# Gamma in four pieces on four partitions, issued beside ScalarE's table load, in an RMSNorm and SiLU kernel

## Chip, cores and metric

The kernel runs on one core of a Trainium2 chip. The metric is the device time of one execution in microseconds (us). Runs of one kernel mostly agree within half a per cent, so each kernel is run several times, in rounds with the kernel before on the same chip. A ratio below compares the fast runs of one kernel with the fast runs of the kernel before in the same rounds, so it is not quite the ratio of the medians quoted; the interval behind it is 95%. With one core a run counts as slow when it is over 1.5% above the fastest of the same kernel. A profiled span is about 1.8 us shorter than the time that the same execution is given.

## The reference

```python
# x: 8 x 1024 x 2048 float32, gamma: 2048 float32
rms = np.sqrt(np.mean(x ** 2, axis=-1, keepdims=True) + eps)
out = gamma * x / rms
return out * (1 / (1 + np.exp(-out)))
```

67.1 MB come in and 67.1 MB go out. Gamma is 8 KB, and every one of the 128 partitions needs a copy of it.

## The kernel before

x is cut into 16 blocks of 128 partitions x 4 rows of 2048 (4.19 MB, 32 KB a partition). Six buffers turn: a block is loaded, scaled in place and stored from the same buffer. Loads are issued by SyncE (SP), stores by ScalarE (ACT). For each block VectorE sums the squares of one row and ScalarE those of three, VectorE makes the inverse root and multiplies by gamma, ScalarE applies SiLU. Gamma arrives as one row on partition 0, in a buffer that the sixth load reuses; TensorE multiplies a column of ones by it, and VectorE copies the result from PSUM, where the matmuls leave it, to a buffer g that every later multiplication reads.

```python
def store(b):
    nc.scalar.dma_start(out=ob[b], in_=blocks[b])
    if b + LEAD < nblk:
        load(b + LEAD)            # LEAD = BUFS = 6: load b+6 waits for store b
...
with tc.manual_schedule():
    grow = pool.tile([P, J * d], f32, name="xt")
    nc.scalar.dma_start(out=grow[0:1, 0:d], in_=...gamma as one row...)
    for b in range(min(LEAD, BUFS - 1)):
        load(b)
    nc.vector.memset(ones, 1.0)                       # ones is 1 x 128
    for c in range(0, d, 512):
        nc.tensor.matmul(junk_v[:, c:c + 512], ones, grow[0:1, c:c + 512], start=True, stop=True)
    nc.vector.tensor_copy(out=g, in_=junk_v)
    load(BUFS - 1)
    ...
    sums(0); rstds[0] = rsqrt(sss[0]); finish(0)
    sums(1); rstds[1] = rsqrt(sss[1])
    for b in range(1, last - 1):
        sums(b + 1, after_first=[b - 1])              # store b-1 goes out after the first sum of block b+1
        finish(b)
        rstds[b + 1] = rsqrt(sss[b + 1])
```

Of the kernel before, what the change touches and what calls it, by code (L numbers as in the profile page):

```python
# [1 line left out]

# [4 lines left out]

ACT = mybir.ActivationFunctionType
ALU = mybir.AluOpType


@with_exitstack
def kernel(
    ctx: ExitStack,
    tc: tile.TileContext,
    x: bass.AP,
    gamma: bass.AP,
    eps: bass.AP,
    out: bass.AP,
):  # L20





    nc = tc.nc
    P = nc.NUM_PARTITIONS
    f32, i32 = mybir.dt.float32, mybir.dt.int32
    x2 = x.flatten_outer_dims()
    o2 = out.flatten_outer_dims()  # L30
    n, d = x2.shape
    J = 4
    BUFS, LEAD = 6, 6
    nblk = n // (P * J)
    xb = x2.rearrange("(b p j) d -> b p (j d)", p=P, j=J)
    ob = o2.rearrange("(b p j) d -> b p (j d)", p=P, j=J)

    singles = ctx.enter_context(tc.tile_pool(name="singles", bufs=1))
    pool = ctx.enter_context(tc.tile_pool(name="pool", bufs=BUFS))
    small = ctx.enter_context(tc.tile_pool(name="small", bufs=2))  # L40
    psum = ctx.enter_context(tc.tile_pool(name="psum", bufs=1, space=bass.MemoryType.PSUM))

    g = singles.tile([P, d], f32)
    ones = singles.tile([1, P], f32)
    junk_a = psum.tile([P, d], f32, name="junk_a")
    junk_v = psum.tile([P, d], f32, name="junk_v")
    blocks, sss, rstds = {}, {}, {}

    def load(b):
        xt = pool.tile([P, J * d], f32, name="xt")  # L50
        nc.sync.dma_start(out=xt, in_=xb[b])
        blocks[b] = xt

    def row(b, j):
        return blocks[b][:, j * d:(j + 1) * d]

    def rsqrt(ss):


        var = small.tile([P, J], f32, name="var")  # L60
        nc.vector.tensor_scalar(out=var, in0=ss, scalar1=1.0 / d, scalar2=float(eps),  # L61
                                op0=ALU.mult, op1=ALU.add)
        y = small.tile([P, J], f32, name="y")
        t = small.tile([P, J], f32, name="t")
        nc.vector.tensor_single_scalar(out=t.bitcast(i32), in_=var.bitcast(i32), scalar=1,  # L65
                                       op=ALU.logical_shift_right)
        nc.vector.tensor_scalar(out=y.bitcast(i32), in0=t.bitcast(i32), scalar1=-1, scalar2=0x5F375A00,  # L67
                                op0=ALU.mult, op1=ALU.add)
        for _ in range(3):
            nc.vector.scalar_tensor_tensor(out=t, in0=y, scalar=-0.5, in1=y, op0=ALU.mult, op1=ALU.mult)  # L70
            nc.vector.tensor_mul(out=t, in0=t, in1=var)  # L71
            nc.vector.scalar_tensor_tensor(out=y, in0=t, scalar=1.5, in1=y, op0=ALU.add, op1=ALU.mult)  # L72
        return y

    def sums(b, after_first=()):


        ss = small.tile([P, J], f32, name="ss")
        nc.vector.tensor_tensor_reduce(  # L79
            out=junk_v, in0=row(b, J - 1), in1=row(b, J - 1), scale=1.0, scalar=0.0,  # L80
            op0=ALU.mult, op1=ALU.add, accum_out=ss[:, J - 1:J])
        for j in range(J - 1):
            nc.scalar.activation(out=junk_a, in_=row(b, j), func=ACT.Square,  # L83
                                 accum_out=ss[:, j:j + 1])
            if j == 0:
                for s in after_first:
                    store(s)
        sss[b] = ss

    def finish(b, pieces=1):  # L90
        for j in range(J):
            nc.vector.tensor_mul(out=row(b, j), in0=row(b, j), in1=g)  # L92
            nc.scalar.activation(out=row(b, j), in_=row(b, j), func=ACT.Silu,  # L93
                                 scale=rstds[b][:, j:j + 1])
            if pieces > 1 and (j + 1) % (J // pieces) == 0:
                w = J // pieces * d
                i = (j + 1) // (J // pieces) - 1
                nc.scalar.dma_start(out=ob[b][:, i * w:(i + 1) * w], in_=blocks[b][:, i * w:(i + 1) * w])  # L98
# [4 lines that stand above are left out]
            load(b + LEAD)  # L103

    with tc.manual_schedule():
        grow = pool.tile([P, J * d], f32, name="xt")
        nc.scalar.dma_start(out=grow[0:1, 0:d],
                            in_=bass.AP(tensor=gamma.tensor, offset=gamma.offset, ap=[[d, 1], gamma.ap[0]]))
        for b in range(min(LEAD, BUFS - 1)):
            load(b)  # L110
        nc.vector.memset(ones, 1.0)  # L111
        for c in range(0, d, 512):
            nc.tensor.matmul(junk_v[:, c:c + 512], ones, grow[0:1, c:c + 512], start=True, stop=True)  # L113
        nc.vector.tensor_copy(out=g, in_=junk_v)  # L114
        load(BUFS - 1)


        last = nblk - 1
        sums(0)
        rstds[0] = rsqrt(sss[0])  # L120
        finish(0)
        sums(1)
        rstds[1] = rsqrt(sss[1])
        for b in range(1, last - 1):
            sums(b + 1, after_first=[b - 1])
            finish(b)
            rstds[b + 1] = rsqrt(sss[b + 1])
        store(last - 2)
        finish(last - 1)
        store(last - 1)  # L130
        sums(last)
        rstds[last] = rsqrt(sss[last])
        finish(last, pieces=2)


# [1 line left out]
_INS = ['x', 'gamma', 'eps']  # L137
_OUTS = [((8, 1024, 2048), 'float32')]

_NUMBERS = {'eps': 9.999999747378752e-06}  # L140


# [26 lines left out]
```

## Time and profile before

| | before |
|---|---|
| time, median of the first 3 runs | 317.92 us (317.8 to 318.91) |
| DMA share between 80 and 240 us | 1.00, at 432 to 433 GB/s |
| busy: VectorE, ScalarE, TensorE | 66%, 70%, 2% |
| gamma in PSUM / in g / first used | 9.7 / 12.0 / 21.6 us |
| first load landed / first store issued | 13.2 / 38.48 us |

The table is read from top to bottom as "what is full, what is early": the transfers are full, and gamma is ready 9.5 us ahead of its first use. The lines themselves stand in the prediction.

### The profile page before, as it was taken

The page shows a single profiled execution, that of the slowest core. Times are in us where ns is not written, and L with a number is a line of the kernel's source. Part 1 is how long each engine was busy: PE and PEld are TensorE (multiplying, and loading weights), DVE is VectorE, ACT ScalarE, POOL GpSimd, SP SyncE. Part 2 cuts the span into 40 slices and gives each one's busy share as a digit, 9 for nine tenths or more (in the row PEclk, how much of TensorE's full clock was granted, in tenths as well). Part 3 has the DMA queues.
Part 4 walks back from the last instruction along what each step waited for, and adds up shares of the span by engine and source line. Part 5 has one row for each costly group of instructions (what it writes and reads, how often), then busy time and mean ns, then how long its engine had stood idle before and what let it go on. Part 6 is the DMA issues. An engine that isn't in the chain of part 4 may idle for free.

```text
span 317.5 us, 603 instructions
## 1 busy us (share of the span) xinstructions
PE 7.2 (2%) x8; PEld 2.5 (1%) x8; DVE 210.3 (66%) x290; ACT 221.3 (70%) x162; POOL 0.2 (0%) x4
## 2 busy tenths in 40 slices
PE   6200000000000000000000000000000000000000
PEld 2000000000000000000000000000000000000000
DVE  0559299999892947839287392974929559946600
ACT  1359989999892947939388393984929659794800
POOL 0000000000000000000000000000000000000000
DMA  8999999999999999999999999999999999999994
GB/s 327 429 433 433 425 392 455 405 454 417 442 430 433 425 438 425 433 446 425 438 425 439 417 442 433 425 458 417 442 417 446 413 446 433 430 446 425 438 411 204
DMA packets 4758, 134.26 MB, mean 423 GB/s; under 512 B 529, under 2 KB 529, under 8 KB 529
## 3 DMA queue, kind: packets, MB, share of 16 engines
q1 hardware_dynamic: 2304, 67.11, 49.4%
q10 hardware_dynamic: 2450, 67.12, 49.0%
q14 instruction: 4, 0.03, 0.0%
HBM read 67.12 MB, written 67.11 MB: 423 GB/s over the span
## 4 chain that ended last, share of the span: by engine, by line
DMA 73%; DVE 11%; ACT 7%; issue 3%; DVEq 1%; ACTq 0%; SPq 0%
DMA xt<-in_x_dram 39%; DMA out_dram<-xt 34%; DVE xt L92 8%; ACT junk_a L83 5%; ACT xt L93 3%; DVE junk_v L79 1%; DVEq L164 1%; DVE t L70 0%; DVE t L71 0%; DVE y L72 0%; DVE t L65 0%; DVE y L67 0%; DVE var L61 0%; ACTq L98 0%; ACTq L101 0%
## 5 line engine op out<-in xcount | busy, mean ns | idle before, releaser
L92 DVE TENSOR_TENSOR xt<-xt,g 128x2048 f32<-128x2048 f32 x64 | 142.3, 2285 | 0.0
L83 ACT ACTIVATE junk_a<-xt 128x2048 f32<-128x2048 f32 x48 | 90.3, 1881 | 65.5 <-DMA xt<-in_x_dram 64.0
L93 ACT ACTIVATE xt<-xt,y 128x2048 f32<-128x2048 f32 x64 | 124.0, 1992 | 13.0 <-DVE xt L92 13.0
L79 DVE CUSTOM_DVE_ANT_0 junk_v<-xt 128x2048 f32<-128x2048 f32 x16 | 36.8, 2299 | 57.5 <-DMA xt<-in_x_dram 57.5
L61 DVE TENSOR_SCALAR var<-ss 128x4 f32<-128x4 f32 x16 | 2.6, 166 | 15.7 <-ACT junk_a L83 15.7
L83 ACT ACTIVATION_READ_ACCUMULATOR junk_a<-xt 128x1 f32 x48 | 9.0, 187 | 0.0
L72 DVE SCALAR_TENSOR_TENSOR y<-t,y 128x4 f32<-128x4 f32 x48 | 7.8, 162 | 1.7
L70 DVE SCALAR_TENSOR_TENSOR t<-y 128x4 f32<-128x4 f32 x48 | 7.8, 162 | 1.7
L71 DVE TENSOR_TENSOR t<-t,var 128x4 f32<-128x4 f32 x48 | 7.8, 162 | 1.6
L114 DVE COPY g<-junk_v 128x2048 f32<-128x2048 f32 x1 | 2.3, 2292 | 8.7 <-PE junk_v L113 8.7
L113 PE MATMUL junk_v<-xt,ones 1*128 1x512 f32 x8 | 7.2, 1072 | 2.5 <-DMA xt<-in_gamma_dram 2.5
L67 DVE TENSOR_SCALAR y<-t 128x4 int32<-128x4 int32 x16 | 2.7, 170 | 0.5
L65 DVE TENSOR_SCALAR t<-var 128x4 int32<-128x4 int32 x16 | 2.7, 170 | 0.5
L113 PEld LDWEIGHTS junk_v<-xt,ones 1*128 1x128 f32 x8 | 2.5, 325 | 5.6 <-issue 5.6
L79 DVE DVE_READ_ACCUMULATOR2_ANT ss<- 128x1 f32 x16 | 2.3, 142 | 0.0
L83 ACT ACT_TABLE_LOAD x1 | 1.3, 1283 | 1.3 <-PEq L150 1.3
L93 ACT ACT_TABLE_LOAD x1 | 1.3, 1283 | 0.0
L111 DVE MEMSET ones<- 1x128 f32 x1 | 0.2, 165 | 0.8 <-PEq L150 0.8
L150 POOL MEMSET const-bfloat16-1.0<- 128x1 bf16 x1 | 0.1, 102 | 0.0
L150 POOL MEMSET const-uint8-127<- 128x1 uint8 x1 | 0.1, 102 | 0.0
L150 POOL MEMSET const-float32-0.0<- 128x1 f32 x1 | 0.1, 100 | 0.2 <-issue 0.2
L150 POOL MEMSET const-float32-1.0<- 128x1 f32 x1 | 0.1, 99 | 0.0
## 6 DMA issues: line engine op xcount, KB each, us to landing
xt<-in_x_dram SPq DMA_DIRECT2D x16, 4096.0 KB, 36.8
out_dram<-xt ACTq DMA_DIRECT2D x15, 4096.0 KB, 40.6
out_dram<-xt ACTq DMA_DIRECT2D x2, 2048.0 KB, 15.4
xt<-in_gamma_dram ACTq DMA_DIRECT2D x1, 8.0 KB
```

The source lines that it names most:

```text
L61: nc.vector.tensor_scalar(out=var, in0=ss, scalar1=1.0 / d, scalar2=float(eps), op0=ALU.mult, op1=ALU.add)
L65: nc.vector.tensor_single_scalar(out=t.bitcast(i32), in_=var.bitcast(i32), scalar=1, op=ALU.logical_shift_right)
L67: nc.vector.tensor_scalar(out=y.bitcast(i32), in0=t.bitcast(i32), scalar1=-1, scalar2=0x5F375A00, op0=ALU.mult, op1=ALU.add)
L70: nc.vector.scalar_tensor_tensor(out=t, in0=y, scalar=-0.5, in1=y, op0=ALU.mult, op1=ALU.mult)
L71: nc.vector.tensor_mul(out=t, in0=t, in1=var)
L72: nc.vector.scalar_tensor_tensor(out=y, in0=t, scalar=1.5, in1=y, op0=ALU.add, op1=ALU.mult)
L79: nc.vector.tensor_tensor_reduce(out=junk_v, in0=row(b, J - 1), in1=row(b, J - 1), scale=1.0, scalar=0.0, op0=ALU.mult, op1=ALU.add, accum ...
L83: nc.scalar.activation(out=junk_a, in_=row(b, j), func=ACT.Square, accum_out=ss[:, j:j + 1])
L92: nc.vector.tensor_mul(out=row(b, j), in0=row(b, j), in1=g)
L93: nc.scalar.activation(out=row(b, j), in_=row(b, j), func=ACT.Silu, scale=rstds[b][:, j:j + 1])
L113: nc.tensor.matmul(junk_v[:, c:c + 512], ones, grow[0:1, c:c + 512], start=True, stop=True)
L164: with _tile.TileContext(nc) as tc:
```

## The change

The intent: let nothing stand ahead of the loads of x at the start, have ScalarE load its table and gamma in the shade of the first load, spread gamma over four partitions and let TensorE broadcast each piece from its own 32-row group.

```diff
-    ones = singles.tile([1, P], f32)
+    ones = singles.tile([P, P], f32)
...
+        Q = 4
+        w = d // Q
         grow = pool.tile([P, J * d], f32, name="xt")
-        nc.scalar.dma_start(out=grow[0:1, 0:d], in_=...one row...)
-        for b in range(min(LEAD, BUFS - 1)):
+        for b in range(BUFS - 1):
             load(b)
         nc.vector.memset(ones, 1.0)
-        for c in range(0, d, 512):
-            nc.tensor.matmul(junk_v[:, c:c + 512], ones, grow[0:1, c:c + 512], start=True, stop=True)
+        nc.scalar.activation(out=junk_a[:, 0:1], in_=ones[:, 0:1], func=ACT.Square)
+        nc.scalar.dma_start(out=grow[0:P:P // Q, 0:w], in_=...4 x 512...)
+        for c in range(Q):
+            k = c * (P // Q)
+            nc.tensor.matmul(junk_v[:, c * w:(c + 1) * w], ones[k:k + 1, :], grow[k:k + 1, 0:w],
+                             start=True, stop=True)
```

More of the change, by code (lines that the diff above doesn't have):

```diff
@@ L105 @@
     with tc.manual_schedule():
+        Q = 4
+        w = d // Q
         grow = pool.tile([P, J * d], f32, name="xt")
-        nc.scalar.dma_start(out=grow[0:1, 0:d],
-                            in_=bass.AP(tensor=gamma.tensor, offset=gamma.offset, ap=[[d, 1], gamma.ap[0]]))
-        for b in range(min(LEAD, BUFS - 1)):
+        for b in range(BUFS - 1):
             load(b)
         nc.vector.memset(ones, 1.0)
-        for c in range(0, d, 512):
-            nc.tensor.matmul(junk_v[:, c:c + 512], ones, grow[0:1, c:c + 512], start=True, stop=True)
+        nc.scalar.activation(out=junk_a[:, 0:1], in_=ones[:, 0:1], func=ACT.Square)
+        nc.scalar.dma_start(out=grow[0:P:P // Q, 0:w],
+                            in_=bass.AP(tensor=gamma.tensor, offset=gamma.offset, ap=[[w, Q], [1, w]]))
+        for c in range(Q):
+            k = c * (P // Q)
+            nc.tensor.matmul(junk_v[:, c * w:(c + 1) * w], ones[k:k + 1, :], grow[k:k + 1, 0:w],
+                             start=True, stop=True)
         nc.vector.tensor_copy(out=g, in_=junk_v)
```

## The prediction

> **What bounds the kernel now.** I read the page's slices first, then the stretches table, then the opening of the timeline, and last the chain of waits and the waits of the load queue. The page's slices of the span:
>
> ```profile
> span 317.5 us, 603 instructions
> ...
> PE   6200000000000000000000000000000000000000
> PEld 2000000000000000000000000000000000000000
> DVE  0559299999892947839287392974929559946600
> ACT  1359989999892947939388393984929659794800
> ...
> DMA  8999999999999999999999999999999999999994
> ...
> HBM read 67.12 MB, written 67.11 MB: 423 GB/s over the span
> ```
>
> One row is full from the second slice to the last but one, and it is the DMA row. VectorE and ScalarE have holes in every phase, TensorE works for two slices out of 40. The stretches of the span (busy time of each engine, clock, DMA share, GB/s) say what lies outside the full part:
>
> ```profile
> 0.00:2.00 2.00, 0.00 (x0) 0.00 (x0) 0.17 (x1) 0.70 (x1) 0.20 (x4) 1.00 0.62 168
> 2.00:40.00 38.00, 7.16 (x8) 2.49 (x8) 18.98 (x29) 23.31 (x19) 0.00 (x0) 1.00 0.99 423
> 80.00:160.00 80.00, 0.00 (x0) 0.00 (x0) 52.65 (x77) 55.37 (x42) 0.00 (x0) 1.00 1.00 432
> 160.00:240.00 80.00, 0.00 (x0) 0.00 (x0) 54.07 (x75) 56.42 (x43) 0.00 (x0) 1.00 1.00 433
> ...
> 313.00:314.00 1.00, 0.00 (x0) 0.00 (x0) 0.00 (x0) 0.00 (x0) 0.00 (x0) 1.00 0.20 82
> 314.00:317.50 3.50, 0.00 (x0) 0.00 (x0) 0.00 (x0) 0.00 (x0) 0.00 (x0) 1.00 0.04 19
> ```
>
> At 433 GB/s the 134.26 MB need 310.1 us, so of 317.5 us only 7.4 lie outside. About 2 are the start before the first packets and about 4 the tail, in which three engines and then one are still busy (82 and 19 GB/s, where 16 engines make 433, 27 each). The trace's packet records agree: a 32 KB packet takes 1.213 us in the median on its engine, and each engine has bytes for 256 of them, 310.5 us. Most engines end near 313.5 us, one at 316.2. I followed the packets of each engine by their ends and starts: the straggler began its first load packet last, 1.0 us after the first one, and had one packet of 2.98 us when loads and stores first mixed. The engine that carried gamma is not the straggler; it ends with the bulk.
>
> The opening of the timeline is where the change acts:
>
> ```profile
> 0.73 9.31 SPq L51 DMA_DIRECT2D xt<-in_x_dram  x6
> 0.74 0.52 ACTq L107 DMA_DIRECT2D xt<-in_gamma_dram  x1
> 1.30 1.28 ACT L83 ACT_TABLE_LOAD   x1 [1.30 <-PEq L150]
> 2.53 7.16 PE L113 MATMUL junk_v<-xt,ones 1*128 1x512 f32 x8 [2.53 <-DMA xt<-in_gamma_dram]
> 9.73 2.29 DVE L114 COPY g<-junk_v 128x2048 f32<-128x2048 f32 x1 [8.75 <-PE junk_v L113]
> 13.18 1.88 ACT L83 ACTIVATE junk_a<-xt 128x2048 f32<-128x2048 f32 x1 [10.60 <-DMA xt<-in_x_dram]
> 13.30 2.30 DVE L79 CUSTOM_DVE_ANT_0 junk_v<-xt 128x2048 f32<-128x2048 f32 x1 [1.29 <-DMA xt<-in_x_dram]
> 19.29 0.17 DVE L61 TENSOR_SCALAR var<-ss 128x4 f32<-128x4 f32 x1 [3.62 <-ACT junk_a L83]
> ```
>
> Gamma is ready in g at 12.02 us, and the first multiplication by it is at 21.55. VectorE's next work after the copy, the sum of squares of block 0, waits for x until 13.30; the block then waits for ScalarE's three sums until 19.27. So gamma is early twice over. The table load is early too: it ends at 2.58, the first activation starts at 13.18. The waits of the load queue close the case:
>
> ```profile
> SPq L51 <- DMA out_dram<-xt: 226.6, 10, 54.3
> ...
> SPq L51 <- PE junk_v L113: 6.2, 1, 6.2
> ```
>
> The sixth load, which reuses gamma's buffer, waits 6.2 us for TensorE and is issued at 9.7 us, but five loads of 4.19 MB at 433 GB/s keep the transfers busy until about 2 + 5 x 9.7 = 50 us. From then on loads wait for stores, that is for bandwidth.
>
> **What the Trainium skill says.** "DMA: Bandwidth & Descriptors", section "Where 436 GB/s comes from", puts the ceiling of a core's 16 engines at 435 GB/s; the trace's 432 to 433 agrees, so nothing is to be gained in the middle. The same page, section "Queues, rings and completion order", says that an engine takes turns between the queues it has work for, a packet at a time. The trace agrees: when the first store joins the loads, its packets on one engine start 2.42 us apart, twice 1.213; and its first packet starts 4.55 us after the issue at 38.48, about 3.6 more than the 0.9 that gamma took from issue (0.74) to its packet (1.65) on an idle chip. A small transfer issued behind loads pays that. Section "Why a DMA increments its semaphore by 16 and not by 1" says that the slowest dimension sets the number of engines, lowest-numbered first: so gamma goes from one engine to four. Gamma's one completion shows before (529 packets below 512 B are 33 large transfers x 16 plus 1). "TensorE: Matmul & The Clock Gate", section "Part 3: Packing small matmuls — row/col tiling", says that matmuls of different row groups run together, 3.07 times faster for four; the trace of before has all on one row, so it shows nothing of it.
>
> **The change part by part.**
> Moved: gamma's issue, from 0.74 us to behind table load and a small activation. The table load no longer has the 0.52 us issue ahead: 0.78 to 2.06. The activation of 128x1 on the ones (filled by 0.98) I put at 0.2 us, as the 128x1 accumulator reads (187 ns): issue at about 2.3. Plus 0.9 + 3.6 queueing: packets at about 6.8. Each piece is 2 KB, at 27 GB/s 0.08 us; the completion follows at once or one load packet (1.2 us) later: landed at 7 to 8.3 us instead of 2.5.
> TensorE: eight passes before, 0.85 us apart (7.16 - 1.19 over 7), 7.16 in all. If passes of one piece stay in turn while neighbouring pieces overlap, it is about five steps, 5 x 0.85 = 4.3 us; without overlap 7.2, with full overlap about 2. So broadcast ends near 12 (10 to 15.5).
> VectorE: copy 2.29, then sum of squares 2.30 + 0.14: block 0's fourth sum is ready near 12 + 4.8 = 16.8 (14.8 to 20.3, but not before 15.7, where x sets it). Needed at 19.27, when ScalarE's third sum is in. Cost to the path 0, at worst 1.0 us of delay for block 0.
> Even that 1.0 doesn't reach the end: it moves the first store from 38.48 to 39.5, and loads alone still fill the engines until about 60 us.
> Sixth load: issued near 12 to 15.5 rather than 9.7, needed in the queue by 50. Cost 0.
> The memset of 128x128 instead of 1x128: the same 128 elements a partition, 0.17 us, cost 0.
> Transfers: gamma's 8 KB packet took 0.45 us on one engine; now four engines carry 0.08 each. That engine gets 0.4 us back, but it is not the one that ends last: gain 0 if so, 0.4 at most.
> Start: the first load's issue took 0.71 us, beside the ACT queue's issue of gamma, later ones 0.33 to 0.46. Alone it could be 0.2 to 0.35 shorter, and the last engines could start sooner. I count 0.3 of gain.
> The order of instructions and of semaphores: stores wait for the store four before in both, and have it by the time their data is there, so no new wait.
> Sum: -0.3 us on 317.92: 317.6.
>
> **Rivals.** First: gamma is starved behind the loads, each engine working off several 1.2 us packets before the 2 KB piece and again before its completion. For it: the 4.55 us of the first store. Against: it would have to land after about 7.1 us with no overlap on TensorE (or 10 with it) to delay block 0, and after more than some 17 us to leave the store so late that engines idle at 60. It would make block 0 late by 1 to 5 us and the time 317.6 to 318.
> Second: the start is what matters. ACT's issue at 0.74 delayed the loads' descriptors, and gamma's packet one engine; all 16 now start by up to 1 us sooner and the straggler ends sooner: 316.6 to 317. For it: the 0.71 us issue and the 1.0 us spread of first packets. Against: the straggler isn't gamma's engine, and first packets take 1.4 to 2.1 us on every engine[...].
> Third: the straggler's 2.98 us packet is chance at the point where loads and stores meet. Moving the first store or the piece's turn could take 1 us away or add one on another engine. The three runs of before spread over 1.1 us (317.8 to 318.91), so such an effect would pass for noise.
>
> **Range and chances.** All rivals lie within 316.5 to 319.0, and so do the runs of before; that is my range for 8 times in 10, with 317.6 in it. Two per cent is 6.4 us, nearly all of the 7.4 us outside the transfers' own time; to lose as much, the engines would have to idle. I give 0.01 to faster, 0.98 to within 2%, 0.01 to slower.
>
> **What would show it.** Right: DMA share 1.00 between 40 and 300 us; gamma landing at 7 to 8.3 us; matmuls closing in less than 7.2 us with overlapping starts; the copy ending before 16.6; first sum of ScalarE near 13; 532 packets below 512 B. The step on the start is wrong if the first load lands at 13.2 or later still; the one on TensorE if eight passes still take 7.2. The whole is wrong if the stretch at 40 to 80 us has a DMA share below 0.97, or if the tail after 313 us grows by more than 2 us.

## The result, and the profile after

| | before | after |
|---|---|---|
| time, median of 6 runs | 318.55 us (317.8 to 319.18) | 318.06 us (317.85 to 319.31) |
| ratio of fast runs | 1 | 0.9996 (95%: 0.9973 to 1.0018) |
| TensorE busy | 7.2 us | 2.1 us |
| gamma in g | 12.0 us | 12.6 us |
| first load landed | 13.2 us | 13.0 us |

Nothing moved that can be told from noise. The page of the changed kernel, span and slices:

```profile
span 316.3 us, 605 instructions
...
PE   0200000000000000000000000000000000000000
...
DMA  8999999999999999999999999999999999999996
...
DMA packets 4764, 134.26 MB, mean 424 GB/s; under 512 B 532, under 2 KB 532, under 8 KB 536
```

TensorE's work went from the first slice into the second and shrank. 532 small packets in place of 529 and four more below 8 KB: gamma now has four data packets and four completions, so it went over four engines. The stretches of the changed kernel (from and to, length, busy us of PE, PEld, DVE, ACT and POOL, clock, DMA share, GB/s):

```profile
2.00:40.00 38.00, 2.09 (x8) 0.55 (x8) 19.09 (x30) 23.04 (x20) 0.00 (x0) 1.00 0.98 421
80.00:160.00 80.00, 0.00 (x0) 0.00 (x0) 52.80 (x76) 55.44 (x42) 0.00 (x0) 1.00 1.00 433
160.00:240.00 80.00, 0.00 (x0) 0.00 (x0) 53.53 (x73) 55.88 (x42) 0.00 (x0) 1.00 1.00 433
...
313.00:314.00 1.00, 0.00 (x0) 0.00 (x0) 0.00 (x0) 0.00 (x0) 0.00 (x0) 1.00 0.20 82
314.00:316.30 2.30, 0.00 (x0) 0.00 (x0) 0.00 (x0) 0.00 (x0) 0.00 (x0) 1.00 0.03 14
```

The middle is as full as before. The span of this profile is 1.2 us shorter, and the last lines show where: the last engine ended at 315.0 us, in the profile of before at 316.2. The median of the 16 engines' ends is 313.57 us after and 313.47 before, so the bulk didn't gain. (The packet records name no engine. Here and below the engines are told apart by following the end of one packet to the start of the next, which is not unique where two packets end together; counts early in the run are safer than what one engine did in all.) The timeline of the changed kernel's opening (start, duration, engine, line, operation, out<-in, count, and in brackets the idle time before and what ended it; SPq and ACTq are the queues on which SyncE and ScalarE issue transfers):

```profile
0.73 1.28 ACT L114 ACT_TABLE_LOAD   x1 [0.73 <-PEq L157]
0.73 9.87 SPq L51 DMA_DIRECT2D xt<-in_x_dram  x6
1.03 1.09 ACTq L115 DMA_DIRECT2D xt<-in_gamma_dram  x1
2.02 0.17 ACT L114 ACTIVATE junk_a<-ones 128x1 f32<-128x1 f32 x1
8.13 2.09 PE L119 MATMUL junk_v<-xt,ones 1*128 1x512 f32 x8 [8.13 <-DMA xt<-in_gamma_dram]
10.28 2.29 DVE L121 COPY g<-junk_v 128x2048 f32<-128x2048 f32 x1 [9.28 <-PE junk_v L119]
13.11 2.30 DVE L79 CUSTOM_DVE_ANT_0 junk_v<-xt 128x2048 f32<-128x2048 f32 x1 [0.54 <-DMA xt<-in_x_dram]
19.15 0.17 DVE L61 TENSOR_SCALAR var<-ss 128x4 f32<-128x4 f32 x1 [3.69 <-ACT junk_a L83]
```

Gamma lands 5.6 us later than before (TensorE starts at 8.13 instead of 2.53), TensorE takes 5.1 us less, and so g is full 0.55 us later: two effects that cancel. VectorE still waits for x at 13.11 and for ScalarE's sums at 19.15. Two things are not as the source reads. The issue of gamma starts at 1.03, while the table load runs until 2.01: ScalarE's queue sends it out without waiting for the work ahead of it, so it isn't behind the table load. And the sixth load's waits, from the waits of the load queue of the changed kernel, are now mostly for gamma's landing:

```profile
SPq L51 <- DMA xt<-in_gamma_dram: 4.9, 1, 4.9
SPq L51 <- PE junk_v L119: 2.2, 1, 2.2
```

### The profile page after: what moved, and what is told of

Same layout as the page of the kernel before. It is cut to its first block, busy times and chain, and to the rows that moved or that the text cites. A ratio compares the mean times of both kernels' runs of the same rounds, so it can differ in the third digit from the quotient of the medians.

```text
span 316.3 us, 605 instructions
## 1 busy us (share of the span) xinstructions
PE 2.1 (1%) x8; PEld 0.5 (0%) x8; DVE 210.3 (66%) x290; ACT 221.4 (70%) x163; POOL 0.2 (0%) x4
## 4 chain that ended last, share of the span: by engine, by line
DMA 73%; DVE 11%; ACT 7%; issue 3%; DVEq 1%; ACTq 0%; SPq 0%
DMA xt<-in_x_dram 40%; DMA out_dram<-xt 33%; DVE xt L92 8%; ACT junk_a L83 5%; ACT xt L93 3%; DVE junk_v L79 1%; DVEq L171 1%; DVE t L71 0%; DVE t L70 0%; DVE y L72 0%; DVE t L65 0%; DVE y L67 0%; DVE var L61 0%; ACTq L98 0%; ACTq L101 0%
## 5 line engine op out<-in xcount | busy, mean ns | idle before, releaser
L119 PE MATMUL junk_v<-xt,ones 1*128 1x512 f32 x8 | 2.1, 1133 | 8.1 <-DMA xt<-in_gamma_dram 8.1
L119 PEld LDWEIGHTS junk_v<-xt,ones 1*128 1x128 f32 x8 | 0.5, 306 | 8.1 <-issue 8.1
```

The costliest lines, as they stand in the source:

```text
L119: nc.tensor.matmul(junk_v[:, c * w:(c + 1) * w], ones[k:k + 1, :], grow[k:k + 1, 0:w], start=True, stop=True)
```

## The experiments

Theory A is the prediction's: the 16 transfer engines set the time by start, rate and end, and gamma has microseconds of slack. Rival B: ScalarE's early issue of gamma held up the first loads, and moving it is a real gain. Rival C: the 1.2 us between the first two profiles is chance. Theory D came up on the way and is told there. The runs fell on four chips, each beside the kernel before on the same chip. All kernels are correct but for no_gamma, which is wrong.

### again: the changed kernel unaltered

> The changed kernel unaltered, for a closer interval and a second trace. Theory A (the 16 transfer engines set the time, gamma has microseconds of slack): ratio to the kernel before 0.999, between 0.997 and 1.001, and the profiled execution within 316.0 to 317.6 us of span, with another engine ending last than in the first trace or the same one for other reasons. Rival B (ACT's early issue of gamma held up the first loads, so moving it is a real gain): ratio 0.996 to 0.998, and the spread of the sixteen first load packets again about 0.5 us against 1.1 before. Rival C (the 1.2 us between the two first profiles is chance): ratio 1.000 within 0.001, and this trace ends anywhere in 316.0 to 317.6.

Measured: 318.5 us (318.01 to 320.49), before 318.62 us; ratio 1.0001 (0.997 to 1.0032). The span was 317.1 us, between the two first profiles, and the first packets of the 16 engines were spread over 0.8 us (0.5 in the first trace, 1.1 before). That speaks for C: the 1.2 us were chance. B's range of 0.996 to 0.998 lies mostly outside the ratio's interval, but not all of it; the next run decides.

### no_gamma: no gamma at all

```diff
-        (ones, small activation, gamma's DMA, four matmuls, copy to g)
+        nc.vector.memset(g, 1.0)
+        nc.scalar.activation(out=junk_a[:, 0:1], in_=g[:, 0:1], func=ACT.Square)
```

> Gamma is not loaded at all, g is filled with ones (wrong result on purpose). It takes away the issue, the packets, the eight TensorE passes, the copy and the sixth load's wait, so it bounds all that gamma's arrival can cost or give. Theory A: ratio to the kernel before 0.998 to 1.001, first load landed at 13.05 us, no more than 0.15 us sooner than with gamma first. Rival B: 0.995 to 0.997, no slower than the changed kernel. If gamma were on the path of block 0, the first multiplication by g would start sooner than 21.4 us; Theory A has it at 21.3 to 21.5.

Measured: 318.48 us, ratio 0.9998 (0.9975 to 1.0021). With gamma's whole path removed, the time is that of before: nothing that is done to make gamma cheaper can show. Rival B's 0.995 to 0.997 fell. Block 0 doesn't start sooner either: the first load lands at 13.07 us (12.96 in the changed kernel), VectorE's step on ScalarE's sums begins at 19.26 (19.15), the first multiplication by g at 21.52 (21.42).

### early_four: the pieces issued first

```diff
         grow = pool.tile([P, J * d], f32, name="xt")
+        nc.scalar.dma_start(out=grow[0:P:P // Q, 0:w], in_=...4 x 512...)
         for b in range(BUFS - 1):
             load(b)
         nc.vector.memset(ones, 1.0)
-        nc.scalar.activation(out=junk_a[:, 0:1], in_=ones[:, 0:1], func=ACT.Square)
-        nc.scalar.dma_start(out=grow[0:P:P // Q, 0:w], in_=...4 x 512...)
```

> Only the four pieces and the four rows on TensorE, with gamma issued first as in the kernel before and without the small activation. Theory A: eight passes take 2.1 us from about 2.6 us, the copy ends near 7 us, and nothing follows from it: ratio 0.998 to 1.001. Rival B: the first load's issue is again near 0.71 us, the first load lands near 13.2 us and the ratio is 1.000, above that of the changed kernel by 0.002 or more.

Measured: 318.59 us, ratio 0.9997 (0.9974 to 1.0019). The time is as expected, the landing is not. Two lines of this kernel's timeline:

```profile
0.73 1.08 ACTq L111 DMA_DIRECT2D xt<-in_gamma_dram  x1
8.12 2.09 PE L118 MATMUL junk_v<-xt,ones 1*128 1x512 f32 x8 [8.12 <-DMA xt<-in_gamma_dram]
```

Issued at 0.73 us, the pieces land no sooner than when issued at 1.03. Nor do the loads suffer from it: the first load's issue takes 0.37 us, as in the changed kernel, and it lands at 12.99 us, where B had 0.71 and 13.2. The issue takes 1.08 us where that of one row took 0.52, and in that time the loads' packets are on the engines. The packet records show the queue: on one of the four engines of the changed kernel: load packets of 1.79, 1.22 and 1.21 us, then gamma's of 0.084 us at 6.04, then one more load packet of 1.21, then the completion at 7.33.

### late_one: one row, issued as late as the pieces

```diff
-        nc.scalar.dma_start(out=grow[0:P:P // Q, 0:w], in_=...4 x 512...)
+        nc.scalar.dma_start(out=grow[0:1, 0:d], in_=...one row...)
-            nc.tensor.matmul(..., ones[k:k + 1, :], grow[k:k + 1, 0:w], ...)
+            nc.tensor.matmul(..., ones[0:1, :], grow[0:1, c * w:(c + 1) * w], ...)
```

> Only the later issue: one 8 KB row behind the table load and the small activation, broadcast from one row. Theory A: gamma lands near 8 us (its packet waits behind three load packets on its engine, the completion behind one more), eight passes take 7.2 us again, the copy ends near 17.6 us, the sum of squares of block 0 near 20.1 us, so block 0's chain is about 0.9 us later than the 19.15 us of the changed kernel, and the first store too; the time doesn't move: ratio 0.998 to 1.001. A theory in which block 0's lateness reaches the end: +0.9 us, ratio 1.002 to 1.004.

Measured: 318.52 us, ratio 0.9998 (0.9975 to 1.0021). Lines of its timeline:

```profile
1.03 0.51 ACTq L115 DMA_DIRECT2D xt<-in_gamma_dram  x1
6.83 7.16 PE L118 MATMUL junk_v<-xt,ones 1*128 1x512 f32 x8 [6.83 <-DMA xt<-in_gamma_dram]
14.03 2.29 DVE L120 COPY g<-junk_v 128x2048 f32<-128x2048 f32 x1 [13.03 <-PE junk_v L118]
19.22 0.17 DVE L61 TENSOR_SCALAR var<-ss 128x4 f32<-128x4 f32 x1 [0.52 <-ACT junk_a L83]
```

The shorter issue put gamma behind two load packets instead of three (its packet at 4.85 us, the completion one load packet later, 6.37), so it landed at 6.8, not near 8, and block 0's lateness came to nothing: the last line waits for ScalarE with 0.52 us to spare, not for VectorE. So this run doesn't test what a late block 0 costs. It does isolate TensorE: the same eight passes take 7.16 us from one row and 2.09 us from four.

### behind_1, behind_2, behind_3: gamma late by a measured dose

```diff
         for b in range(BUFS - 1):
             load(b)
+            if b == 1:                      # 2 and 3 in the other two
+                nc.sync.dma_start(out=grow[0:P:P // Q, 0:w], in_=...4 x 512...)
-        (small activation and gamma's issue on ScalarE)
```

> A measured dose of lateness: the four pieces are issued on the load queue behind the second load of x, in the same order on each engine. Gamma should land about 23 us, g be full near 27.7 us (15 later than in the changed kernel), and the first store be issued about 21.6 us after that, near 49.3 us instead of 38.3. Theory A: loads alone keep the engines full until about 60 us, so the time stays: ratio 0.997 to 1.003. A theory in which gamma's arrival is on the path: +11 to +15 us, ratio 1.035 to 1.047.

> The same behind the third load. Gamma lands near 32.8 us, g full near 37.4, first store issued near 59 us, where the loads run out (2 + 6 x 9.7 = 60.2 us). Theory A: the edge of the slack; the store just takes over from the loads, but the seventh load starts only after the whole first store has landed, alone, so a bubble of 1.5 to 2.5 us: +1.5 to +3.5 us, ratio 1.005 to 1.011. Gamma on the path: +21 to +25 us, ratio 1.066 to 1.079.

> The same behind the fourth load. Gamma lands near 42.5 us, g full near 47.1, first store issued near 68.7 us. Theory A: past the slack: engines idle from about 60.2 to 69.6 us, then the bubble of about 2 us at the seventh load: +10 to +13 us, ratio 1.031 to 1.041, and the DMA share of the stretch 60 to 70 us near 0.1. Gamma on the path: +30 to +35 us, ratio 1.094 to 1.110.

| run | g full | first store issued | idle time around 60 to 90 us, mean of the 16 engines | time | ratio |
|---|---|---|---|---|---|
| after | 12.6 us | 38.34 us | none | 318.06 | 0.9996 |
| behind_1 | 27.1 us | 48.77 us | none | 319.11 | 1.0027 (1.0004 to 1.0051) |
| behind_2 | 37.0 us | 58.69 us | 2.5 us | 320.61 | 1.0073 (1.0044 to 1.0101) |
| behind_3 | 46.7 us | 68.41 us | 8.6 us, then 3.0 | 330.0 | 1.0366 (1.0342 to 1.0389) |

Stretches of behind_3 show the hole:

```profile
60.00:68.00 8.00, 0.00 (x0) 0.00 (x0) 2.64 (x3) 7.74 (x7) 0.00 (x0) 1.00 0.00 0
68.00:70.00 2.00, 0.00 (x0) 0.00 (x0) 1.33 (x9) 1.97 (x3) 0.00 (x0) 1.00 0.61 262
```

All three lie in theory A's ranges. Gamma may come 14.5 us later for 0.3%; past the point at 60 us where the six loads have run out, lateness shows. The 8.6 + 3.0 us of idle engines match behind_3's 11.6 us (330.0 - 318.39, before in the same rounds).

### behind_1b: the first dose again

> The kernel with gamma behind the second load again, since its first result (1.0027, interval 1.0004 to 1.0051) is not explained: its trace has no idle transfer engine, only packets that take 0.4 us more per engine in sum. If that was chance, the ratio is 0.998 to 1.001 now; if lateness inside the slack has a small cost of its own, it is 1.002 to 1.004 again.

Measured: 319.18 us, ratio 1.0017 (1.0001 to 1.0034). On another chip the small cost is there again, between the two ranges set for it, with an interval that just leaves out 1. In both traces no engine idles, and load packets between 80 and 100 us sum to 0.40 and 0.44 us over their 1.213 us per engine, where the changed kernel has 0.04. They follow a stretch in which the load queue was empty (69.9 to 76.8 us in the first). So loads that set in again beside running stores had slow packets there. That these make up the whole of the 0.4 to 0.7 us is not shown.

### start_late: g first, then the loads

```diff
     def load(b):
         xt = pool.tile([P, J * d], f32, name="xt")
+        if b == 0:
+            nc.vector.memset(xt[:, 0:1], 0.0)    # on VectorE behind the copy to g
         nc.sync.dma_start(out=xt, in_=xb[b])
...
-        (five loads, small activation)
         nc.scalar.dma_start(out=grow[0:P:P // Q, 0:w], in_=...4 x 512...)
         ...
         nc.vector.tensor_copy(out=g, in_=junk_v)
-        load(BUFS - 1)
+        for b in range(BUFS):
+            load(b)
```

> Gamma's four pieces go out first on an idle chip, and the first load of x is held back until g is full. This tells what is on the path: g is full sooner than in the changed kernel, the loads start later. With nothing ahead of them the pieces should land near 2.7 us (8.1 us in the changed kernel and in the run with the pieces issued first), g be full near 7.2 us, and the first load be issued near 7.5 us instead of 0.73. Theory A, in which only the transfers' start, rate and end count: the time grows by the shift of the first load, +6.7 us, ratio 1.021. A theory in which gamma's landing matters: no growth, as g is full 5 us sooner.

Measured: 329.63 us, ratio 1.035 (1.0323 to 1.0377). With nothing ahead of them the pieces' packets ran at 2.1 to 2.4 us and TensorE started at 2.90, as expected: the 5 us that gamma took longer in the change are queueing behind load packets. But the time grew by 11 us, not by the 6.7 us that the first load was held back. Slow load packets came all through the run: 12% of them took over 1.26 us, in the changed kernel 2.4%; the median stayed at 1.213. That was not in theory A.

### behind_0: a small dose

The edit is that of behind_1 with `b == 0`.

> A smaller dose: the pieces behind the first load of x. Gamma lands near 13 us, g is full near 17.4 us (4.8 later than in the changed kernel), the first store is issued near 39 us, since the sum of squares of block 0 ends 0.6 us after ScalarE's third sum. Theory A: ratio 0.998 to 1.001. If lateness inside the slack costs in proportion, a third of what the dose behind the second load costs: 1.001.

Measured: 333.91 us, single runs 323.06, 331.39, 333.75, 334.06, 334.09 and 340.75. Five of the six count as slow; no ratio is given. But the fastest of them is above all 11 runs of before in the same rounds (317.81 to 319.41), at the same clock of 1.0, and none of those 11 was slow, so the loss goes with the kernel and not with the chip. The expectation failed badly: g 4.9 us later than in the changed kernel, and the first store 0.9, cost more than g 14.5 us later and the first store 10.4 (behind_1). g was full at 17.5 us and the first store issued at 39.22, as expected. So what else had changed?

In the packet records I counted, engine by engine, the load packets that each had worked off before its first store packet, and, as "excess", the time of load and store packets beyond 1.213 us each:

| trace | first store, us after the first load's issue | load packets ahead of the first store, by engine | excess packet time per engine | state |
|---|---|---|---|---|
| before | 37.75 | 33 (15 engines), 34 (1) | 1.7 us | fast |
| after | 37.61 | 33 (15), 34 (1) | 1.7 us | fast |
| again | 37.62 | 33 (12), 34 (4) | 2.1 us | fast |
| early_four | 37.58 | 33 (16) | 1.8 us | fast |
| behind_0 | 38.49 | 33 (2), 34 (14) | 6.9 us | slow |
| start_late | 38.78 | 34 (15), 35 (1) | 5.1 us | fast |
| behind_1 | 48.04 | 41 to 43 | 2.1 us | fast |

From there on loads and stores take turns on each engine, so that distance stays. Load packets begun less store packets begun, averaged over the engines and over 80 to 240 us (a count that needs no engine's name), is 32.5 to 32.7 in before, after, again and early_four, 33.3 in behind_0, 33.4 in start_late, and 36.0 in behind_1, where the distance shrank. This gave theory D: the distance between the two streams, in whole packets, decides how long the packets take, and 34 at the start is a bad one. The excess is not all of behind_0's loss: it has 5.2 us more of it than the changed kernel, and its profiled run took 16 us longer. The rest is at the end: from 300 us on the DMA share falls to 0.81 and 0.73, and two engines end at 331 us, the others at 323.

### store_later: only the first store moved

```diff
     def sums(b, after_first=()):
         ...
+        if b == 2:
+            nc.scalar.activation(out=junk_a[:, 0:960], in_=row(1, 0)[:, 0:960], func=ACT.Square)
         for j in range(J - 1):
             ...                                  # store 0 goes out after the first of these
```

> The changed kernel with one extra activation of about 1 us ahead of ScalarE's sums of block 2, so that only the first store goes out about 1 us later (39.3 us instead of 38.34); gamma and the loads are untouched. In every fast trace so far each engine had worked off 33 load packets before its first store packet, in the two slow ones (loads held back; gamma behind the first load) 34. Theory D (the position of the store stream in the load stream decides how long later packets take, and gamma only matters through it): 34 load packets ahead of the first store, packets over 1.213 us all through, ratio 1.02 to 1.07. Theory A as predicted (a microsecond of delay of the first store is hidden): ratio 0.998 to 1.002.

Measured: fast runs 324.21, 324.25 and 324.27 us, slow ones 331.77, 334.73 and 335.32, before 318.21 us (317.79 to 319.42); ratio of the fast runs alone 1.018 (1.0156 to 1.0203). The profile is of a fast run. The added activation and the first store in its timeline, then two stretches of the middle and the tail:

```profile
38.44 0.97 ACT L83 ACTIVATE junk_a<-xt 128x960 f32<-128x960 f32 x1
39.45 0.36 ACTq L103 DMA_DIRECT2D out_dram<-xt  x1
```

```profile
80.00:160.00 80.00, 0.00 (x0) 0.00 (x0) 52.46 (x76) 55.22 (x41) 0.00 (x0) 1.00 1.00 425
160.00:240.00 80.00, 0.00 (x0) 0.00 (x0) 51.95 (x72) 54.31 (x40) 0.00 (x0) 1.00 1.00 424
...
312.00:322.40 10.40, 0.00 (x0) 0.00 (x0) 0.00 (x0) 0.00 (x0) 0.00 (x0) 1.00 0.47 202
```

In the middle the DMA share is 1.00, as before, and the rate 424 to 425 GB/s instead of 433: no engine idles, but 14% of the load packets between 80 and 240 us take over 1.26 us (0.3% in the changed kernel); the median packet still takes 1.213. All 16 engines had 34 load packets ahead of the first store, the average distance was 33.4, the excess 5.2 us per engine, 4.9 of it in loads. These longer packets are some 3.5 us an engine more than in the changed kernel, of a loss of 6. The median engine ends 2.8 us later than in the changed kernel (316.39 us, 313.57), the last one 6.1 us later (321.17, 315.03): the slow packets fall unevenly on the engines, and the last line shows the tail in which most of them have finished. One microsecond of work in the shade of the transfers costs 6 us in fast runs and up to 17 in slow ones. Theory A's range is left in every run.

### start_late_33: the late start, with the distance put back

```diff
 (start_late)
         nc.vector.memset(ones, 1.0)
+        nc.scalar.activation(out=junk_a[:, 0:1], in_=ones[:, 0:1], func=ACT.Square)
```

> The kernel that holds the loads back until g is full, with the small activation added that loads ScalarE's table early. The table load of 1.28 us stood in block 0's chain there (it started when x had landed); taking it out puts the first store at about 44.9 us, 37.5 after the first load's issue as in the changed kernel (37.6), so 33 load packets ahead of it again. Theory D with A: the slow packets vanish and what is left is the shift of the first load alone, +6.7 us, ratio 1.020 to 1.022, and under 2.1 us of excess packet time per engine instead of 5.1. If the slow packets came from the late start itself or from anything else in that kernel: again 1.032 to 1.038.

Measured: 325.55 us, ratio 1.0219 (1.0195 to 1.0243). From its timeline the loads' start and the first store, then two stretches:

```profile
7.41 2.91 SPq L53 DMA_DIRECT2D xt<-in_x_dram  x6
44.98 0.36 ACTq L103 DMA_DIRECT2D out_dram<-xt  x1
```

```profile
80.00:160.00 80.00, 0.00 (x0) 0.00 (x0) 58.55 (x87) 61.26 (x44) 0.00 (x0) 1.00 1.01 433
160.00:240.00 80.00, 0.00 (x0) 0.00 (x0) 52.11 (x73) 54.80 (x41) 0.00 (x0) 1.00 1.00 432
```

44.98 - 7.41 = 37.57 us between the first load's issue and the first store's, 33 load packets ahead on 12 engines and 34 on four (average distance 32.7), an excess of 1.9 us, and 432 to 433 GB/s again. The time is 7.0 us above before (0.0219 x 318.4), where the first load was held back by 7.41 - 0.73 = 6.7. So a small activation that takes a 1.28 us table load out of block 0's chain gave some 4 us (329.63 to 325.55, on two chips; ratios 1.035 and 1.0219), in a kernel whose transfers don't idle once they have begun.

No experiment pointed to a kernel faster than both; with gamma's path removed altogether the time stayed at 318.5 us.

## Why the prediction was right, and where it wasn't

**The bound and the time: right.** 317.6 us were predicted, 318.06 measured, ratio 0.9996, DMA share 1.00 from 40 to 300 us. no_gamma shows the whole path of gamma to be worth nothing, which is the strongest form of the claim.

**Gamma's landing: right in time, in part by luck.** 7 to 8.3 us were predicted, and TensorE starts at 8.13. The issue was put at 2.3 us behind the activation; it came at 1.03. The wait from there to the packets was put at 4.5 us; it took 5.0 to 5.3 (1.03 to 6.04 and 6.35), then one load packet to the completions, the last at 7.64, and 0.5 us more to TensorE's start. The errors made up for each other. What sets the landing is the queue on the engines, three load packets and then one more, as early_four and start_late show.

**TensorE: right in kind, mis-sized.** Five steps of 0.85 us, 4.3 us, were put down, with neighbouring pieces overlapping; it measured 2.09 us, the "about 2" that the prediction gave for full overlap. late_one shows that the rows do it, 7.16 against 2.09 us.

**VectorE and the sixth load: right.** The copy ends at 12.6 us (16.6 was the limit), block 0's chain isn't touched, the sixth load goes out at about 10.3 us, sooner than the 12 to 15.5 put down, and far ahead of its need at 50.

**The gain of 0.3 us at the start: a misreading.** It rested on "the first load's issue took 0.71 us, beside the ACT queue's issue of gamma". The 0.71 us issue of that trace is the third load's, at 1.63 us. The first load's took 0.37 us with gamma's issue beside it, and 0.37 after, so there was nothing to gain there. The first load lands 0.2 us sooner in the profile, but the median end of the engines is 0.1 us later, and no ratio can tell 0.3 us. Which engine the straggler is, and when it began, doesn't come out uniquely either: another way of following the packets gives another engine. The second rival (B above) fell with no_gamma, and the range that the third rival gave to chance holds for the runs of both kernels.

**"Even that 1.0 doesn't reach the end": wrong.** This step, and with it the first rival's "317.6 to 318" for a block 0 late by 1 to 5 us, failed. It wasn't needed, as the lateness came out as 0. The argument was that loads alone fill the engines until 60 us, so the first store may move. They do, but store_later moved it by 1.1 us and lost 6 us or more: the store's place among the load packets went from 33 to 34. Half wrong was that losing 2% needs idle engines: store_later loses 1.8%, somewhat over half of it through longer packets at a DMA share of 1.00 and the rest in a ragged end. The range held because both kernels keep their first store at 38.3 to 38.5 us, on the good side of a step that lies between there and 39.2. That was luck as far as the prediction goes, which allowed 1.0 us of delay and saw no step: behind_0, with g full 5 us later and the first store 0.9, took 4 to 22 us over the median of before. Wrong, too, is the first rival's "more than some 17 us" as the landing from which engines idle at 60: it is too low. The first store at 38.48 has some 21.5 us until 60, and those come on top of the 7 to 10 us at which block 0 begins to be late, so about 29 to 32 us. In behind_1 gamma sets TensorE going at 22.63 us and no engine idles; in behind_2, at 32.55, engines idle for 2.5 us.

**What stays open.** That the place of the first store among the loads decides is shown by moving it one way in store_later and back in start_late_33, the one with gamma's path and the loads' start as in the changed kernel, the other with both as in start_late. The count and the time go together in these runs (37.6 to 37.8 us for 33, 38.5 to 38.8 for 34), so that whole packets matter, and not the microsecond, is not shown. Nor does an engine's own count settle it: in again and start_late_33 four engines had 34 and the excess was 2.1 and 1.9 us, while in behind_0 the two engines that had 33 were, as far as their packets can be followed, as slow as the rest. Why 34 is bad when most engines have it, and 33 and the 36 at which behind_1 settles are not, isn't shown. "DMA: Bandwidth & Descriptors", section "Latency and other measured facts", tells of copies that lose half of their rate at a row pitch in HBM of some large powers of two (4 MiB), and calls the cause, streams of the partitions in lock step, an inference. The pitch here is 32 KB, and the two streams are one of reads and one of writes; whether their addresses get in each other's way in a like manner is a guess, as no run of this case tests addresses. Nor is it shown why store_later and behind_0 each have faster and slower runs among them; of each only one run has a profile.

## What to carry to other kernels

A transfer that is early stays worthless to improve, and taking it out altogether is the cheapest way to find out. Where transfers fill the span, look not only at their share but at the time of one packet: the same full row hid a rate 2% lower here, and a microsecond of shaded work may decide it by shifting one stream against another. Before shifting a first store in such a kernel, count the packets ahead of it, and measure the neighbours of the place it has.

## What the Trainium skill lacked or had wrong

- "DMA: Bandwidth & Descriptors", section "Queues, rings and completion order", has the turns between queues but not their price for a small transfer: behind running 32 KB load packets a 2 KB piece waited for three of them and its completion for one more, so that TensorE started 7.1 us after the issue (1.03 to 8.13), against 2.2 us on idle engines (0.73 to 2.90). The records here change queue after each 32 KB record; how many descriptors one holds they don't tell, so they can't be set against the 9 to 17 that the page gives as typical of a turn.
- The same page has nothing on the distance between a load and a store stream that take turns: 33 packets gave 432 to 433 GB/s between 80 and 240 us, 34 gave 421 to 429 (store_later 424 to 425), all at a DMA share of 1.00. Nor on a stream's first packets: 1.4 to 2.1 us at the start of before and after instead of 1.213.
- The same page, section "Issuing engines are not separate DMA queues", calls the time of an issue usually small beside the transfer itself: here it was 1.09 us for 4 x 2 KB against 0.52 us for 1 x 8 KB, in start_late half of the 2.2 us from issue to TensorE's start, and the four pieces fell behind one more load packet than the row did (early_four's and the changed kernel's start of TensorE at 8.1 us, late_one's at 6.8).
- "TensorE: Matmul & The Clock Gate", section "Part 3: Packing small matmuls — row/col tiling", gives 3.07 times for four row groups (32 rows, 512 columns each); these float32 passes, of one row and two to a group, gained 3.4 times (7.16 to 2.09 us).
